# Output products of two feed-forward stages: earlier scalings, additions spread over the steps, a fourth weight buffer, and the last tile in two banks

## The chip, the cores and the metric

One core of a Trainium2 chip runs the whole kernel. The metric is the time of one execution on the device in microseconds, the median of several runs. The core has five engines that run beside each other and wait for one another by semaphores: TensorE (PE in the profile, with its weight loads as PEld), VectorE (DVE), ScalarE (ACT), GpSimd (POOL) and SyncE (SP). SP only issues DMAs here, in order, from one queue; a DMA whose buffer isn't free yet holds up those behind it.

## The reference

One layer of a hybrid model: 512 tokens of width 1024, feed-forward width 2816, all in float32.

```python
mod = jax.nn.silu(c) @ w_ada + b_ada
sh1, sc1, g1, sh2, sc2, g2, sh3, sc3, g3 = [m[:, None, :] for m in jnp.split(mod, N_MOD, axis=-1)]

u = rms_norm(x, ffn1_norm_g) * (1 + sc1) + sh1
x = x + 0.5 * g1 * swiglu(u, ffn1_w_in, ffn1_w_out)     # swiglu: (silu(a) * b) @ w_out, [a b] = u @ w_in
...
x = x + g2 * (merged @ w_out)                           # mLSTM and attention with a forget gate, merged
u = rms_norm(x, ffn2_norm_g) * (1 + sc3) + sh3
x = x + 0.5 * g3 * swiglu(u, ffn2_w_in, ffn2_w_out)
```

The change concerns the two products with `ffn1_w_out` and `ffn2_w_out` (512 x 2816 by 2816 x 1024), and the line that scales their results by 0.5 g and adds them onto x. The two stages are called FFN1 and FFN2 below.

## The kernel before

**Exactness.** TensorE multiplies a rounded kind of float32. So every operand is split in a high half (`wh`, `A`: a copy by ScalarE, L102 for weights) and a low half (`wl`, `Ra`, `Rb`, `Rl`: what is left, a subtraction by VectorE, L104 for weights). One product is three matmuls, `mm3`: high by high (L127), high by low (L128 and L129, named for their place, each with one low half). In the rows, L128 of the output products reads `wl` and L129 a low half of the activations.

**The output product.** `pair_out` computes h @ w_out with seven products for a 2 x 2 block of matrices instead of eight (Strassen and Winograd's scheme). The 22 blocks of 128 rows of w_out form NP = 11 pairs, and sums of weight blocks that the scheme needs stand ready in DRAM (`ws`). There are two sweeps over the pairs.

The first sweep sums three products in PSUM banks and ends with P1 = the first of them, U2 = P1 + the second (L573) and U4 = U2 + the third (L575), each for two tiles of 128 tokens (`tb` 0 and 1), 128 x 512. These six tiles belong to the result: scaled by 0.5 g they are added onto x.

The second sweep sums four products, Z and Y in banks named t, X and W in banks named g, each for two values of tb. It has 8 steps, one for each of pairs 0 to 7, of 24 matmuls. A step needs two weight tiles of 128 x 1024 (512 KB): `c` out of w_out for Z and Y, and `d` out of `ws` for X and W. Each is loaded by SP into a buffer `raw` (there are 3, used in turn, L92), and split by ScalarE into `wh` and by VectorE into `wl` (4 buffers each). After that, pairs 8, 9 and 10 (`tail = 3`) are done bank by bank: `close` does the remaining 9 matmuls of one bank, so that the banks are finished one after the other and not all at the end. Their d tiles are loaded early, in steps 3, 5 and 7, into buffers that are free by then (`early`, `we`, L544 to L546); their c tiles, c8 to c10, follow behind step 7's in the raw buffers.

**x.** It has four tiles of 128 tokens by two halves of 512 columns. They are loaded in the source's steps 3 to 6 (L621), two a step, from the input in FFN1 and from `x_d` in FFN2. In the source's steps 6 and 7, P1, U2 and U4 are scaled (`scaled`, L597, into a buffer `rs`) and added (`onto`, L600), U4's onto two tiles. When a bank is closed, its sum is scaled and added likewise (X's onto both halves of its tile).

**The end of the stages.** FFN1 hands `pair_out` a function `end`, which closes the banks in an order written by hand and goes on to the next normalization. FFN2 closes X, Z, W and Y in a loop over "XZYW" (X, Z, Y, W), tb 0 and 1 each, and stores each finished tile of 128 x 512 (256 KB, L607): eight stores, the last after W, tb = 1.

**What sets the order.** A scheduler (the Tile framework's) orders the instructions of each engine by the program's dependences and its own estimates; each engine then runs its list in order. So the source's order is a starting point, and the same change of the source can move other instructions too. The buffer named `xn` (one, 128 x 1024) holds the activations' rest `R` of the last pair in FFN1, until L482 has split it, and in FFN2 a sum that a side computation (`ada_row`) builds up until about 1126 us.

Of the kernel before, what the change touches and what calls it, by code (L numbers as in the profile page):

```python
# [11 lines left out]
F32 = mybir.dt.float32  # L12
# [8 lines left out]
P = 128  # L21
# [23 lines left out]
MUL, ADD, SUB, MAX, MIN = ALU.mult, ALU.add, ALU.subtract, ALU.max, ALU.min  # L45


class Layer:
# [478 lines left out]
    def pair_out(self, w, v, hp, tp, x_src, end=None):  # L527

        nc = self.nc
        V = nc.vector.tensor_tensor  # L530
        NP = NJ // 2
        slots = iter([f"{a}{k}" for k in range(NK) for a in ("uh", "ul")])
        new = lambda n: self.up.tile([P, 512], F32, name=self.nm(n), tag=next(slots))
        sh = [P, 2, 512]
        def two(*src):

            n = 2 // len(src)
            t = self.raw(sh, [(lambda t, i=i: t[:, i:i + n, :] if n > 1 else t[:, i, :], a) for i, a in enumerate(src)])
            return self.split(t, sh)
        def early(src, n):  # L540

            hi, lo = [hp.tile(sh, F32R, name=self.nm("we"), tag=f"A{n + i}", bufs=1) for i in range(2)]
            t = lo.bitcast(F32)
            nc.sync.dma_start(t, src)  # L544
            nc.scalar.activation(hi, t, AF.Copy)
            V(lo, t, hi, op=SUB)  # L546
            return hi, lo
        both = lambda r: w[r * P:(r + 1) * P, :].rearrange("p (h n) -> p h n", h=2)
        def one(src):
            t = self.tmp(tp, "raw1")  # L550
            nc.sync.dma_start(t, src)
            return self.split(t, [P, 512])
        def mm(ps, tb, a, b, start, stop):
            s = slice(tb * P, (tb + 1) * P)
            self.mm3(ps[tb], a[0][:, s], a[1][:, s], b[0], b[1], start, stop)

        Z, Y = [[self.tbank() for _ in range(2)] for _ in range(2)]
        X = [self.gbank() for _ in range(2)]
        for i in range(NP):
            wh, wl = two(w[2 * i * P:(2 * i + 1) * P, 0:512], self.ws[i][:, 0, :])  # L560
            w2 = one(self.ws[i][:, 3, :])
            self.tick()
            A1 = self.A1[i]
            for ps, n, b in ((Z, 0, (wh[:, 0, :], wl[:, 0, :])), (X, 2, w2), (Y, 1, (wh[:, 1, :], wl[:, 1, :]))):
                for tb in range(2):
                    mm(ps, tb, (A1[:, n, :], A1[:, 3 + n, :]), b, i == 0, i == NP - 1)
            if i:
                self.pair_split(i - 1, hp, tp)
        P1, U2, U4 = [[new(n) for _ in range(2)] for n in ("P1", "U2", "U4")]
        for tb in range(2):  # L570
            nc.scalar.activation(P1[tb], Z[tb], AF.Copy)
        for tb in range(2):
            V(U2[tb], X[tb], P1[tb], op=ADD)  # L573
        for tb in range(2):
            V(U4[tb], Y[tb], U2[tb], op=ADD)  # L575
        self.pair_split(NP - 1, hp, tp)

        X, W = [[self.gbank() for _ in range(2)] for _ in range(2)]
        Z, Y = [[self.tbank() for _ in range(2)] for _ in range(2)]
        banks = {"Z": Z, "Y": Y, "X": X, "W": W}  # L580
        def prepare(i, d=None):
            c = two(both(2 * i + 1))
            d = d or two(self.ws[i][:, 1:3, :])
            A2 = self.A2[i]
            a = lambda n: (A2[0][:, n, :], A2[1 + n // 2][:, n % 2, :])
            b = lambda n: ((c, d)[n // 2][0][:, n % 2, :], (c, d)[n // 2][1][:, n % 2, :])
            return {"Z": (a(0), b(0)), "Y": (a(3), b(1)), "X": (a(2), b(2)), "W": (a(1), b(3))}
        step = lambda n, tb, i, o: mm(banks[n], tb, *o[n], i == 0, i == NP - 1)
        if end:
            g = [self.mod_bcast(v, h, tp) for h in range(2)]  # L590
        else:
            g = [new("gb") for _ in range(2)]
            for h in range(2):
                nc.sync.dma_start(g[h], self.mod_d[v:v + 1, h * 512:(h + 1) * 512].to_broadcast([P, 512]))
        def scaled(src, half, t=None):
            t = self.tmp(tp, "rs") if t is None else t
            self.pin(nc.vector.scalar_tensor_tensor(t, src, 0.5, g[half], op0=MUL, op1=MUL))  # L597
            return t
        def onto(tb, half, t):
            self.pin(V(self.x[tb][half], self.x[tb][half], t, op=ADD))  # L600
        def add(src, half, tbs):
            t = scaled(src, half)
            for tb in tbs:
                onto(tb, half, t)
            return t
        def store(tb, half):
            nc.sync.dma_start(self.out[0, tb * P:(tb + 1) * P, half * 512:(half + 1) * 512], self.x[tb][half])  # L607
        tail, ds = 3, []
        for i in range(NP - tail):
            o = prepare(i)  # L610
            if i % 2 and i > 1:
                n = NP - tail + len(ds)
                ds.append(early(self.ws[n][:, 1:3, :], i - 3))
            for n in ("XZWY" if i == 0 else "ZYXW"):
                for tb in range(2):
                    step(n, tb, i, o)
            if i == 3:
                self.x_tiles()
            if 3 <= i < 7:
                for h in range(2):  # L620
                    nc.sync.dma_start(self.x[i - 3][h], x_src[(i - 3) * P:(i - 2) * P, h * 512:(h + 1) * 512])  # L621
            if i in (6, 7):
                tb = i - 6
                add(P1[tb], 0, (tb,))
                add(U2[tb], 0, (tb + 2,))
                add(U4[tb], 1, (tb, tb + 2))
        def close(n, tb):
            ps = banks[n][tb]
            for i, o in enumerate(os):
                step(n, tb, NP - tail + i, o)  # L630
            return ps
        place = lambda n, tb: {"Z": (0, tb), "Y": (1, tb), "W": (0, tb + 2)}[n]
        os = [prepare(NP - tail + n, d) for n, d in enumerate(ds)]
        if end:
            end(close, scaled, onto)
            return

        for n in "XZYW":
            for tb in range(2):
                ps = close(n, tb)  # L640
                if n == "X":
                    add(ps, 1, (tb + 2,))
                    add(ps, 0, (tb + 2,))
                    store(tb + 2, 1)
                else:
                    half, q = place(n, tb)
                    add(ps, half, (q,))
                    store(q, half)
# [940 lines left out]
```

## Time and profile before

| | us |
|---|---|
| median of 3 runs | 1327.01 |
| lowest and highest | 1326.8 and 1328.08 |
| profiled execution | 1328.68 |
| its span in the profile | 1326.9 |
| second sweep, FFN1: first matmul | 315.13 |
| second sweep, FFN2: first matmul | 1260.44 |
| last matmul, start | 1321.69 |
| last store, issue | 1323.6 |

The granted clock of TensorE is 1.0 over the span. A row of a timeline has the start in us, the duration in us, the engine, the line, the operation, out<-in with names less their numbers, the shapes, and in brackets the idle time of the engine ahead of it with what ended it. A row can hold several equal instructions in sequence (x2, x3); its duration then covers them all. On TensorE consecutive matmuls overlap, so their pace is read from the starts. A row of a group has, behind the bar, the busy time in us and the mean in ns of one, and behind a second bar the idle time of the engine just ahead. A row of DMA issues has the count, the size of one, and the median us from issue to landing.

### The profile page before, as it was taken

The page shows a single profiled execution, that of the slowest core. Times are in us where ns is not written, and L with a number is a line of the kernel's source. Part 1 is how long each engine was busy: PE and PEld are TensorE (multiplying, and loading weights), DVE is VectorE, ACT ScalarE, POOL GpSimd, SP SyncE. Part 2 cuts the span into 40 slices and gives each one's busy share as a digit, 9 for nine tenths or more (in the row PEclk, how much of TensorE's full clock was granted, in tenths as well). Part 3 has the DMA queues.
Part 4 walks back from the last instruction along what each step waited for, and adds up shares of the span by engine and source line. Part 5 has one row for each costly group of instructions (what it writes and reads, how often), then busy time and mean ns, then how long its engine had stood idle before and what let it go on. Part 6 is the DMA issues. An engine that isn't in the chain of part 4 may idle for free.

```text
span 1326.9 us, 17767 instructions
## 1 busy us (share of the span) xinstructions
PE 1308.3 (99%) x6332; PEld 1091.9 (82%) x6332; DVE 959.9 (72%) x1740; ACT 622.6 (47%) x1038; POOL 43.8 (3%) x65
## 2 busy tenths in 40 slices
PE   7999999999999999999999999999999999999998
PEld 6788888888789888888888788888788888888886
DVE  6877777467788687887887778677577656635777
ACT  5533232355476555566566666334263223223742
POOL 1000000000010101000000000003010000000000
PEclk9999999999999999999999999999999999999999
DMA  9899978464845334533342536687429768624574
GB/s 291 265 325 306 315 269 280 127 194 155 291 133 139 110 108 130 159 103 111 91 122 76 170 96 204 214 256 227 155 92 339 264 235 277 210 97 140 170 260 152
DMA packets 204345, 254.18 MB, mean 192 GB/s; under 512 B 14993, under 2 KB 146481, under 8 KB 204257
## 3 DMA queue, kind: packets, MB, share of 16 engines
q1 hardware_dynamic: 203872, 252.98, 59.9%
q8 instruction: 50, 0.82, 0.2%
q14 instruction: 39, 0.31, 0.1%
q0 software_dynamic: 320, 0.06, 0.0%
q10 hardware_dynamic: 64, 0.02, 0.0%
HBM read 217.28 MB, written 35.72 MB: 191 GB/s over the span
## 4 chain that ended last, share of the span: by engine, by line
PE 91%; DVE 4%; ACT 2%; DMA 2%; issue 1%; POOL 0%; SPq 0%; ACTq 0%; DVEq 0%; POOLq 0%
PE g L127 23%; PE g L129 23%; PE g L128 23%; PE t L128 4%; PE t L127 4%; PE t L129 4%; PE g L825 2%; PE t L1208 1%; PE t L1178 1%; DMA x<-x_d 1%; DVE wl L104 1%; PE t L1149 1%; PE t L825 1%; PE t L1150 1%; ACT wh L102 0%
## 5 line engine op out<-in xcount | busy, mean ns | idle before, releaser
L102 ACT ACTIVATE wh<-raw 128x1024 fp32r<-128x1024 f32 (+2 forms) x250 | 253.9, 1018 | 383.0 <-PE g L128 118.4
L104 DVE TENSOR_TENSOR wl<-raw,wh 128x1024 fp32r<-128x1024 f32 (+2 forms) x250 | 292.9, 1174 | 178.0 <-ACT wh L102 154.8
L128 PE MATMUL g<-ul,wh 128*128 128x512 f32 (+1 forms) x912 | 348.1, 383 | 1.0 <-POOL ul L267 1.0
L127 PE MATMUL g<-uh,wh 128*128 128x512 f32 (+1 forms) x912 | 348.5, 384 | 0.0
L129 PE MATMUL g<-uh,wl 128*128 128x512 f32 (+1 forms) x912 | 348.2, 382 | 0.0
L128 PEld LDWEIGHTS g<-ul,wh 128*128 128x128 f32 x912 | 171.3, 188 | 34.3 <-POOL ul L267 1.8
L129 PEld LDWEIGHTS g<-uh,wl 128*128 128x128 f32 x912 | 171.4, 188 | 33.2
L127 PEld LDWEIGHTS g<-uh,wh 128*128 128x128 f32 x912 | 171.0, 188 | 32.8 <-issue 0.6
L325 DVE SCALAR_TENSOR_TENSOR acc<-raw,ccol,acc 128x512 f32<-128x512 f32 (+1 forms) x70 | 66.8, 975 | 43.0 <-DMA raw<-in_w_ada_dram 42.6
L127 PE MATMUL g<-wh,uh 128*128 128x512 f32 (+1 forms) x256 | 97.4, 380 | 0.0
L129 PE MATMUL g<-wh,ul 128*128 128x512 f32 (+1 forms) x256 | 96.6, 377 | 0.0
L128 PE MATMUL g<-wl,uh 128*128 128x512 f32 (+1 forms) x256 | 96.4, 377 | 0.0
L128 PE MATMUL t<-wl,A 128*128 128x512 f32 x176 | 69.3, 394 | 1.7 <-DVE wl L104 1.6
L127 PE MATMUL t<-wh,A 128*128 128x512 f32 x176 | 69.3, 394 | 0.1
L129 PEld LDWEIGHTS g<-wh,ul 128*128 128x128 f32 x256 | 48.2, 188 | 9.0
L127 PEld LDWEIGHTS g<-wh,uh 128*128 128x128 f32 x256 | 48.2, 188 | 8.7 <-DVE tk L1046 0.5
L128 PEld LDWEIGHTS g<-wl,uh 128*128 128x128 f32 x256 | 48.2, 188 | 8.3
L127 PE MATMUL g<-yh,wh 128*128 128x512 f32 x128 | 50.4, 394 | 0.0
L129 PE MATMUL g<-yh,wl 128*128 128x512 f32 x128 | 50.2, 392 | 0.0
L128 PE MATMUL g<-yl,wh 128*128 128x512 f32 x128 | 49.7, 388 | 0.0
L455 ACT ACTIVATE A<-E 128x768 fp32r<-128x768 f32 x22 | 18.6, 846 | 56.5 <-DVE E L454 50.6
L1160 ACT ACTIVATE S<-S,mn 128x128 f32<-128x128 f32 (+1 forms) x64 | 35.5, 556 | 16.1 <-DVE mn L1152 9.9
(343 smaller groups left out, 2187.5 us busy)
## 6 DMA issues: line engine op xcount, KB each, us to landing
raw<-in_ffn_w_in_dram SPq DMA_DIRECT2D x82, 512.0 KB, 5.2
raw<-in_w_ada_dram SPq DMA_DIRECT2D x56, 512.0 KB, 5.1
raw<-in_w_mix_dram SPq DMA_DIRECT2D x46, 512.0 KB, 4.3
sa<-in_ffn_w_out_dram SPq DMA_DIRECT2D x22, 512.0 KB, 5.4
sb<-in_ffn_w_out_dram SPq DMA_DIRECT2D x44, 256.0 KB, 5.9
ws<-sa SPq DMA_DIRECT2D x22, 512.0 KB, 4.5
ws<-sb SPq DMA_DIRECT2D x44, 256.0 KB, 4.1
raw<-ws SPq DMA_DIRECT2D x44, 256.0 KB, 3.4
```

Source lines behind the costliest of these rows:

```text
L102: nc.scalar.activation(hi, src, AF.Copy)
L104: self.last_lo = nc.vector.tensor_tensor(lo, src, hi, op=SUB)
L127: pin(mm(ps, lh, rh, start=start, stop=False))
L128: pin(mm(ps, lh, rl, start=False, stop=False))
L129: self.last_mm = pin(mm(ps, ll, rh, start=False, stop=stop))
L325: nc.vector.scalar_tensor_tensor(a, r[:, s], c, a, op0=MUL, op1=ADD)
L455: nc.scalar.activation(A1[:, 0:3, :], E[:, 0:3, :], AF.Copy)
L825: pin(nc.tensor.matmul(acc_ps[b], (wl if p == 1 else wh)[:, b % 2, s], self.ul[k] if p == 2 else self.uh[k], start=k == 0 and p == 0, stop ...
L1149: nc.tensor.matmul(ps[:, :w], q[:, s], k[:, :w], start=True, stop=False)
L1150: nc.tensor.matmul(ps[:, :w], q[:, s], kl[:, :w], start=False, stop=True)
L1160: nc.scalar.activation(S[:, ws], S[:, ws], AF.Exp, scale=-1.0, bias=m, accum_out=sm[:, qb:qb + 1])
L1178: tr = lambda b, c, qb, kb: nc.tensor.transpose(b[:, c:c + P], S[:, P_OFF[qb] + kb * P:P_OFF[qb] + (kb + 1) * P], self.ident)
```

## The change

1. A fourth buffer. For odd pairs, the d tile goes into the buffer `xn` (`two_x`) and no longer into a raw buffer. Even d tiles and all c tiles keep the three raw buffers.
2. P1, U2 and U4 are scaled in place in steps 0, 1 and 2, two operations a step. From step 4 on, each step adds two of them onto x: step i onto the two halves of the token tile i - 4.
3. In FFN2 only: bank W of tb = 1 ends after step 7 and is scaled and added onto its tile of x ahead of the closings. Its remaining three pairs are done last, in two new banks of 256 columns each, with a scaling, an addition and a store (128 KB) of their own. These are 18 matmuls of 256 columns in place of 9 of 512.

In all TensorE gets 9 instructions more, VectorE 4 and SP one store; ScalarE and GpSimd keep theirs.

```diff
+        def two_x(src):
+            t = tp.tile(sh, F32, name=self.nm("raw"), tag="xn", bufs=1)
+            nc.sync.dma_start(t, src)
+            return self.split(t, sh)
...
-        banks = {"Z": Z, "Y": Y, "X": X, "W": W}
+        banks, tail = {"Z": Z, "Y": Y, "X": X, "W": W}, 3
...
-            d = d or two(self.ws[i][:, 1:3, :])
+            d = d or (two_x if i % 2 else two)(self.ws[i][:, 1:3, :])
...
-        step = lambda n, tb, i, o: mm(banks[n], tb, *o[n], i == 0, i == NP - 1)
+        step = lambda n, tb, i, o: mm(banks[n], tb, *o[n], i == 0, i == NP - (1 if end or n != "W" or not tb else 1 + tail))
...
-            if i in (6, 7):
-                tb = i - 6
-                add(P1[tb], 0, (tb,))
-                add(U2[tb], 0, (tb + 2,))
-                add(U4[tb], 1, (tb, tb + 2))
+            for src, half in ((P1, 0), (U2, 0), (U4, 1))[i:i + 1]:
+                for tb in range(2):
+                    scaled(src[tb], half, src[tb])
+            if i >= 4:
+                tb = i - 4
+                onto(tb, 0, (P1, U2)[tb // 2][tb % 2])
+                onto(tb, 1, U4[tb % 2])
...
+        add(W[1], 0, (3,))
         for n in "XZYW":
             for tb in range(2):
+                if n == "W" and tb:
+                    for c in (slice(0, 256), slice(256, 512)):
+                        ps, x, r = self.gbank((P, 256)), self.x[3][0][:, c], slice(P, 2 * P)
+                        for i, o in enumerate(os):
+                            a, b = o[n]
+                            self.mm3(ps, a[0][:, r], a[1][:, r], b[0][:, c], b[1][:, c], i == 0, i == tail - 1)
+                        t = self.tmp(tp, "rs")[:, :256]
+                        nc.vector.scalar_tensor_tensor(t, ps, 0.5, g[0][:, c], op0=MUL, op1=MUL)
+                        V(x, x, t, op=ADD)
+                        nc.sync.dma_start(self.out[0, 3 * P:4 * P, c], x)
+                    continue
                 ps = close(n, tb)
```

The lines behind the change move by 4 to 18: what was L546 is L550, L597 is L601, L600 is L604, L621 is L625; `two_x` loads at L542, and the last tile's two parts are scaled at L654, added at L655 and stored at L656.

Three places show what this does to the engines' lists. Names carry numbers here that tell the tiles apart.

VectorE in FFN2's second sweep, steps 5 and 6, before. `wl_11907` is the low half of d5, `wl_11944` that of c6, `wl_11950` that of d6; `we` is an early d tile, `x_11854` and `x_11855` are the halves of token tile 2, and `x_11853`, `x_11856` and `x_11857` those of tiles 1 and 3.

```order
L104 TENSOR_TENSOR wl_11907<-raw_11904,wh_11906 128x1024
L600 TENSOR_TENSOR x_11854<-x_11854,rs_11982 128x512
L546 TENSOR_TENSOR we_11911<-we_11911,we_11910 128x1024
L600 TENSOR_TENSOR x_11855<-x_11855,rs_11985 128x512
L597 TENSOR_SCALAR rs_12036<-U_2228_11675,gb_11698 128x512
L600 TENSOR_TENSOR x_11853<-x_11853,rs_12036 128x512
L104 TENSOR_TENSOR wl_11944<-raw_11941,wh_11943 128x1024
L600 TENSOR_TENSOR x_11856<-x_11856,rs_12033 128x512
L104 TENSOR_TENSOR wl_11950<-raw_11947,wh_11949 128x1024
```

The same place now, where d5, c6 and d6 are `wl_11909`, `wl_11948` and `wl_11954`:

```order
L104 TENSOR_TENSOR wl_11909<-raw_11906,wh_11908 128x1024
L104 TENSOR_TENSOR wl_11948<-raw_11945,wh_11947 128x1024
L550 TENSOR_TENSOR we_11913<-we_11913,we_11912 128x1024
L604 TENSOR_TENSOR x_11854<-x_11854,U_2219_11666 128x512
L604 TENSOR_TENSOR x_11855<-x_11855,U_2221_11668 128x512
L604 TENSOR_TENSOR x_11857<-x_11857,U_2222_11669 128x512
L104 TENSOR_TENSOR wl_11954<-raw_11951,wh_11953 128x1024
L604 TENSOR_TENSOR x_11856<-x_11856,U_2220_11667 128x512
```

c6 has moved ahead of the early tile and of all additions; three additions stand between it and d6. In step 4 likewise one addition stands ahead of c4's `wl` (two of them and the early tile before), and two more and the early tile between c4's and d4's.

TensorE at the start of FFN1's second sweep, before; `wl_2801` is d0's low half, `wl_2795` c0's, g_2780 and g_2781 are X's banks, t_2784 is Z's first.

```order
L127 MATMUL g_2780<-wh_2800,A_444_2406 128x512
L127 MATMUL g_2781<-wh_2800,A_444_2406 128x512
L127 MATMUL t_2784<-wh_2794,A_444_2406 128x512
L128 MATMUL t_2784<-wl_2795,A_444_2406 128x512
L129 MATMUL t_2784<-wh_2794,Rl_2407 128x512
```

And now:

```order
L127 MATMUL g_2780<-wh_2800,A_444_2406 128x512
L127 MATMUL g_2781<-wh_2800,A_444_2406 128x512
L127 MATMUL t_2784<-wh_2794,A_444_2406 128x512
L128 MATMUL g_2780<-wl_2801,A_444_2406 128x512
L129 MATMUL g_2780<-wh_2800,Rl_2407 128x512
```

The low half of d0 is read by the fourth matmul; before, it was the eighteenth. FFN2's sweep begins in the same order now.

SP's queue in FFN1, the loads of steps 1 to 3, before: c1, d1, c2, d2, c3, d3.

```order
L92 DMA raw_2828<-in_ffn_w_out_dram 128x1024
L92 DMA raw_2834<-ws_742 128x1024
L92 DMA raw_2864<-in_ffn_w_out_dram 128x1024
L92 DMA raw_2870<-ws_743 128x1024
L92 DMA raw_2900<-in_ffn_w_out_dram 128x1024
L92 DMA raw_2906<-ws_744 128x1024
```

And now:

```order
L92 DMA raw_2830<-in_ffn_w_out_dram 128x1024
L92 DMA raw_2868<-in_ffn_w_out_dram 128x1024
L92 DMA raw_2874<-ws_743 128x1024
L542 DMA raw_2836<-ws_742 128x1024
L92 DMA raw_2906<-in_ffn_w_out_dram 128x1024
L542 DMA raw_2912<-ws_744 128x1024
```

d1 (`raw_2836`) has gone behind c2 and d2, and c3 stands behind it.

More of the change, by code (lines that the diff above doesn't have):

```diff
@@ L607, in store @@
             nc.sync.dma_start(self.out[0, tb * P:(tb + 1) * P, half * 512:(half + 1) * 512], self.x[tb][half])
-        tail, ds = 3, []
+        ds = []
         for i in range(NP - tail):
```

## The prediction

> **What bounds the kernel now.** I began with the page's first and fourth parts: how busy each engine is, and which engine the chain of waits runs through.
>
> ```profile
> PE 1308.3 (99%) x6332; PEld 1091.9 (82%) x6332; DVE 959.9 (72%) x1740; ACT 622.6 (47%) x1038; POOL 43.8 (3%) x65
> PE 91%; DVE 4%; ACT 2%; DMA 2%; issue 1%; POOL 0%; SPq 0%; ACTq 0%; DVEq 0%; POOLq 0%
> L128 PE MATMUL t<-wl,A 128*128 128x512 f32 x176 | 69.3, 394 | 1.7 <-DVE wl L104 1.6
> ```
>
> TensorE sets the end: 99% busy, 91% of the chain. The change adds a little to it and removes nothing from it, so it can only gain where TensorE waits, and behind its last matmul. The groups by line show a wait in the output products: the matmuls of L128 on the t banks idle for VectorE's low half `wl` (third row; L127 is high by high, L128 uses `wl`). That sum counts idle time alone. What a stall costs is the gap between the starts of two matmuls, less the steady gap. TensorE's timeline around the two stalls of FFN2's second sweep:
>
> ```profile
> 1282.26 0.39 PE L127 MATMUL t<-wh,A 128*128 128x512 f32 x1
> 1282.78 0.50 PE L128 MATMUL t<-wl,A 128*128 128x512 f32 x1
> 1283.12 0.40 PE L129 MATMUL t<-wh,Ra 128*128 128x512 f32 x1
> ...
> 1293.61 0.39 PE L127 MATMUL t<-wh,A 128*128 128x512 f32 x1
> 1294.79 0.50 PE L128 MATMUL t<-wl,A 128*128 128x512 f32 x1 [0.80 <-DVE wl L104]
> ```
>
> Undisturbed, matmuls of this sweep start 0.227 us apart (1321.01 to 1321.69 are three gaps, in the rows of the tail below). At c4 (step 4) the second matmul starts 0.52 behind the first, and the third 0.34 behind that: 0.29 + 0.11 = 0.40 lost. At c6 it is 1.18 - 0.227 = 0.95, with the same 0.11 for the restart 1.06. FFN2 loses 1.46 us. VectorE's timeline says why:
>
> ```profile
> 1278.46 0.69 DVE L600 TENSOR_TENSOR x<-x,rs 128x512 f32<-128x512 f32 x1 [1.47 <-DMA x<-x_d]
> ...
> 1281.50 1.23 DVE L104 TENSOR_TENSOR wl<-raw,wh 128x1024 fp32r<-128x1024 f32 x1
> ...
> 1289.84 0.69 DVE L600 TENSOR_TENSOR x<-x,rs 128x512 f32<-128x512 f32 x1 [0.63 <-DMA x<-x_d]
> 1290.45 1.22 DVE L546 TENSOR_TENSOR we<-we,we 128x1024 fp32r<-128x1024 f32 x1
> ...
> 1293.52 1.22 DVE L104 TENSOR_TENSOR wl<-raw,wh 128x1024 fp32r<-128x1024 f32 x1
> ```
>
> VectorE works in order. Ahead of c4's `wl` (1281.50) and c6's (1293.52) stand additions onto x that wait for a load of x, 1.47 and 0.63 us. In front of c6 the run from 1289.84 to 1293.52 is four 0.69 operations on x and one 1.22 split; `wl` ends at 1294.74, TensorE starts at 1294.79.
>
> FFN1's second sweep loses its time at c10, the last weight tile: TensorE, VectorE, SP's queue and ScalarE.
>
> ```profile
> 360.63 0.39 PE L127 MATMUL t<-wh,A 128*128 128x512 f32 x1
> ...
> 361.10 0.40 PE L129 MATMUL t<-wh,Ra 128*128 128x512 f32 x1
> 361.56 0.50 PE L127 MATMUL t<-wh,A 128*128 128x512 f32 x1
> 362.82 0.50 PE L128 MATMUL t<-wl,A 128*128 128x512 f32 x1 [0.76 <-DVE wl L104]
> ...
> 350.44 6.77 SPq L92 DMA_DIRECT2D raw<-in_ffn_w_out_dram  x3
> ...
> 355.62 1.23 DVE L104 TENSOR_TENSOR wl<-raw,wh 128x1024 fp32r<-128x1024 f32 x1 [2.79 <-ACT wh L102]
> 356.82 1.23 DVE L546 TENSOR_TENSOR we<-we,we 128x1024 fp32r<-128x1024 f32 x1
> 361.54 1.22 DVE L104 TENSOR_TENSOR wl<-raw,wh 128x1024 fp32r<-128x1024 f32 x1 [0.89 <-ACT wh L102]
> ...
> 360.44 1.06 ACT L102 ACTIVATE wh<-raw 128x1024 fp32r<-128x1024 f32 x1 [1.05 <-DMA raw<-in_ffn_w_out_dram]
> ```
>
> Here the steady gap is 0.233 (two from 360.63 to 361.10). The gaps of 0.46 and 1.26 and the restart lose 0.23 + 1.03 + 0.10 = 1.36 us. Backwards: c10's `wl` starts 361.54, its `wh` 360.44 after a wait for the load. SP's row covers the loads of c8, c9 and c10, from 350.44 to 357.21; the last is issued at 356.87, right behind d7's `wl` (355.62 + 1.23), because d7 holds the raw buffer that c10 takes.
>
> The tail, TensorE, VectorE and the stores:
>
> ```profile
> 1321.01 0.39 PE L129 MATMUL g<-we,Ra 128*128 128x512 f32 x1
> ...
> 1321.69 0.39 PE L129 MATMUL g<-we,Ra 128*128 128x512 f32 x1
> 1322.12 0.69 DVE L597 SCALAR_TENSOR_TENSOR rs<-g,gb 128x512 f32<-128x512 f32 x1 [0.62 <-PE g L129]
> 1322.84 0.69 DVE L600 TENSOR_TENSOR x<-x,rs 128x512 f32<-128x512 f32 x1
> ...
> out_dram<-x SPq DMA_DIRECT2D x8, 256.0 KB, 2.0
> ```
>
> From the last matmul's end (1322.08) to the span's end (1326.9) pass 4.82 us: a scaling and an addition of 0.69 each, the store's 2.0 and the small steps between them.
>
> **The change part by part.**
>
> *FFN2's stalls.* c6's `wl` now stands ahead of every addition of its step (front part, VectorE's order), and only one addition stands ahead of c4's. The scalings between them are gone from there. So neither tile waits for x ahead of its `wl`, or only behind one addition: gain 1.46. From the other side: three additions now stand ahead of d4's and of d6's `wl`. TensorE uses a d tile only 12 matmuls (2.7 us) into a step, so 1.47 of waiting for x fits there. Bounds 0 to -1.46; I take -1.46: the tile that is needed first no longer queues behind the load that comes last.
>
> *FFN1's stall.* With d7 in the fourth buffer, c10 takes c7's raw buffer. c7's split is over some 4 us before d7's (d7's `wl` waited 2.79 us), so the load is issued about 353 and is there in time. Then VectorE binds: from 355.62 it still has d7, early d10, c8, c9 and c10 to split, at 1.2 each, and c10 ends at 355.62 + 4 x 1.20 + 1.23 = 361.65. Undisturbed TensorE needs it at 361.56. Some 0.15 of the stall is left if d7's `wl` stays where it is: -1.2. Bounds 0 (the chain is not shortened) and -1.36.
>
> *New margins at the sweep's start.*
>
> ```profile
> 313.17 0.69 DVE L597 SCALAR_TENSOR_TENSOR rs<-P,gb 128x512 f32<-128x512 f32 x1
> 313.77 1.28 DVE L573 TENSOR_TENSOR U<-g,P 128x512 f32<-128x512 f32 x2
> 315.83 0.39 PE L128 MATMUL t<-wl,A 128*128 128x512 f32 x1
> ...
> 316.76 0.69 DVE L482 TENSOR_TENSOR Rb<-R,A 128x512 fp32r<-128x512 f32 x1
> 318.65 0.33 SPq L92 DMA_DIRECT2D raw<-in_ffn_w_out_dram  x1
> 322.20 1.06 ACT L102 ACTIVATE wh<-raw 128x1024 fp32r<-128x1024 f32 x1 [4.76 <-DMA raw<-in_ffn_w_out_dram]
> 324.47 0.39 PE L128 MATMUL g<-wl,A 128*128 128x512 f32 x1
> ```
>
> TensorE's new order needs d0's `wl` as its fourth matmul, which is at 315.83. The scaling at 313.17 goes, the two U2 move up 0.6 to end at 314.4, and `wl` behind them ends at 315.7: just in time, 0 to +0.2. d1 is now loaded into the buffer of R's last pair, free only when that is split. By these rows this ends at 317.45; one `wl` (1.22) now comes before it and a scaling (0.6) no longer does, so about 318.1. A load here took 3.55 from issue to use (318.65, 322.20): there at 321.8, `wh` to 322.9, `wl` to 324.1, needed at 324.47. 0 to +0.5. In FFN2 that buffer has long been idle, so there d1 comes earlier than now. I take +0.1 for all of this.
>
> *Work that only moves.* Six scalings a sweep (0.69 each) go into its steps 0 to 2, two a step, behind the `wl` that TensorE needs next; their number stays. FFN2 adds W[1]'s scaling and addition ahead of X's reading on VectorE, 1.38 us. They can start when step 7 is over, and X's first closing takes 9 x 0.227 = 2.04 after that, so they are covered: 0. Without the cover X is read and stored up to 1.4 later, which the closings of Z, W and Y (some 12 us) hide again. SP issues one store more, behind all others.
>
> *The tail.* Nine matmuls of 512 columns become eighteen of 256. Matmuls of 256 columns run in the mix stage, and VectorE has operations of half the size; below them a store of 128 KB from the page's DMA issues:
>
> ```profile
> 399.24 0.28 PE L1398 MATMUL g<-uh,wl 128*128 128x256 f32 x1
> 399.36 0.28 PE L1397 MATMUL g<-uh,wh 128*128 128x256 f32 x1
> ...
> L751 DVE SCALAR_TENSOR_TENSOR ac<-ar,ccol,ac 128x256 f32<-128x256 f32 x49 | 23.7, 483 | 1.3
> L457 DVE TENSOR_TENSOR Rb<-E 128x256 f32<-128x256 f32 x21 | 8.9, 422 | 0.4
> ...
> h_d<-hn SPq DMA_DIRECT2D x16, 128.0 KB, 1.8
> ```
>
> At 0.12 apart they take 2.16 instead of 2.04: +0.12. Each has its own weight load; on average one takes 1091.9 / 6332 = 0.172, and if nothing hid it the eighteen would take 3.10, +1.06. I take the row of the same shape, where the loads are hidden. VectorE's 0.69 + 0.69 becomes 0.48 + 0.42: -0.48. The last store halves; 256 KB landed in 2.0 (above), 128 KB elsewhere in 1.8: -0.2, bounds 0 and -1.0. Together -0.56, bounds +0.58 and -1.36.
>
> The Trainium skill ("TensorE: Matmul & The Clock Gate", section "Back-to-back issue gap") has a stream of weight load and matmul at some 81 ns for 128 columns and 131 ns for 512. Between them, an estimate from that page, 256 columns stand at about 98 ns: 1.76 for the eighteen against 1.18 for the nine, +0.58 in place of +0.12, which would make the time 1324.4. The trace doesn't agree with its 512-column figure (0.227 here against 0.131), so I keep the rows.
>
> *Sum.* -1.46 - 1.2 + 0.1 - 0.56 = -3.1. The profiled execution took 1328.68 us (span 1326.9, 1.78 around it), 1.67 above the median of the three runs. The steps have the same lengths in both, so I take the sum off the median: 1327.01 - 3.1 = **1323.9**. What a measurement can tell from no change here is about 0.2%, 2.65 us: faster means below 1324.36.
>
> **The rivals.**
>
> *FFN1 gives it back.* The fifth split in VectorE's row of splits binds, or c10's load arrives late all the same. For it: the split is ready 0.1 us late as it is, and three loads come close upon each other from 350 on. Against it: c10's load gets 4 us. Then 1327.01 - 1.46 + 0.1 - 0.56 = 1325.1.
>
> *The x wait moves.* d4's or d6's `wl` waits behind three additions whose x comes late. For it: VectorE waited 1.47 for x, and weight loads of 512 KB are issued around the loads of x. Against it: 2.7 us of slack. It would keep FFN2's 1.46: 1325.4.
>
> *Single fourth buffer, slower.* Every second d tile goes through one buffer. d3 can't be requested until d1's `wl` is done, at 324.1, and is needed two steps of 24 matmuls later, 324.47 + 11.2 = 335.7. Less 1.06 and 1.22 for the splits this leaves 9.3 us for the load, which also stands in SP's queue behind the loads ahead of it.
>
> ```profile
> raw<-ws SPq DMA_DIRECT2D x7, 512.0 KB, 7.2
> ```
>
> These are the loads of d in FFN2's second sweep (DMA issues of that stretch): 7.2 us in the median, 2 us in hand. For it: a median leaves half of them above it. It decides from 9.3 us on: at 11 us d3, d5 and d7 would each stall 1.7 in both sweeps, +10.2 - 3.1, about 1334; at 10.5 about 1331.
>
> **How the numbers follow.** The forecast has 0.60, with a range of its own of 1323.1 to 1324.8; about eight tenths of that (0.48) lie under 1324.36. FFN1 gives it back 0.18, the x wait moves 0.13: both within 0.2%. The single buffer has 0.08, slower. The last 0.01 is a larger gain. So faster 0.49, same 0.43, slower 0.08. For 8 in 10: 1322.8 (tail at its best bound) to 1326.0, which leaves out the single buffer and a second failed term.
>
> **What would show it.** TensorE's timeline: no gap over 0.3 at c4, c6 and c10; the group of L128 on the t banks idle near 0.1 instead of 1.7. SP: c10's load issued about 353 in FFN1. VectorE: no wait for `x_d` ahead of a `wl` that TensorE needs next. The last 18 matmuls 0.12 apart and about 4.1 us from their end to the span's. Gaps at L128 on the g banks, on odd steps, would speak for the single buffer; one at FFN1's step 1 for the late d1. Were the second sweeps as long as before with these gaps closed, the reading of the bound would be wrong.

## The result, and the profile after

| | before | changed |
|---|---|---|
| median of 22 runs, us | 1327.66 | 1325.23 |
| lowest to highest, us | 1325.45 to 1329.57 | 1324.66 to 1327.27 |
| ratio, with its 95% interval | | 0.9983 (0.9977 to 0.9989) |
| profiled execution, us | 1328.68 | 1325.80 |
| its span, us | 1326.9 | 1324.0 |

The ratio is 2.3 us of 1327.66, with an interval of 1.5 to 3.1: faster, but by less than the 0.2% that the prediction set as its bound, and 0.8 less than the 3.1 it forecast. In these runs the changed kernel also spreads less.

The page and the group of L128 on the t banks, changed kernel:

```profile
PE 91%; DVE 4%; ACT 2%; DMA 1%; issue 1%; POOL 0%; ACTq 0%; POOLq 0%; DVEq 0%
L128 PE MATMUL t<-wl,A 128*128 128x512 f32 x176 | 69.1, 393 | 0.0
```

The idle time before that group was 1.7 us and is 0. TensorE's timeline of the changed kernel at the three places, c10 in FFN1, c4 and c6 in FFN2:

```profile
360.81 0.39 PE L127 MATMUL t<-wh,A 128*128 128x512 f32 x1
361.04 0.40 PE L128 MATMUL t<-wl,A 128*128 128x512 f32 x1
...
1281.63 0.39 PE L127 MATMUL t<-wh,A 128*128 128x512 f32 x1
1281.85 0.39 PE L128 MATMUL t<-wl,A 128*128 128x512 f32 x1
...
1292.51 0.39 PE L127 MATMUL t<-wh,A 128*128 128x512 f32 x1
1292.73 0.39 PE L128 MATMUL t<-wl,A 128*128 128x512 f32 x1
```

Gaps of 0.23, 0.22 and 0.22, the steady pace; before they were 1.26, 0.52 and 1.18. One small gap is new, at the start of FFN2's second sweep, at d0's low half:

```profile
1260.07 0.39 PE L127 MATMUL t<-wh,A 128*128 128x512 f32 x1
1260.41 0.50 PE L128 MATMUL g<-wl,A 128*128 128x512 f32 x1
1260.74 0.39 PE L129 MATMUL g<-wh,Rl 128*128 128x512 f32 x1
```

Gaps of 0.34 and 0.33 instead of 0.227: 0.22 lost, where the prediction gave 0 to 0.2. FFN1's sweep starts with half of that, 0.10.

The tail: of the kernel before, TensorE's first matmul of the last tile; of the changed kernel, TensorE's first and last matmul of the split tile, VectorE's last two operations, and the two stores (time to issue, first and last issue):

```profile
1319.88 0.39 PE L127 MATMUL g<-we,A 128*128 128x512 f32 x1
...
1317.67 0.28 PE L127 MATMUL g<-we,A 128*128 128x256 f32 x1
1319.70 0.28 PE L129 MATMUL g<-we,Ra 128*128 128x256 f32 x1
...
1320.02 0.42 DVE L654 SCALAR_TENSOR_TENSOR rs<-g,gb 128x256 f32<-128x256 f32 x1
1320.47 0.42 DVE L655 TENSOR_TENSOR x<-x,rs 128x256 f32<-128x256 f32 x1
...
L656 SPq DMA_DIRECT2D out_dram<-x x2: 332/332/332, 1320.1 to 1320.9; - x2
```

Seventeen gaps of the changed kernel take 2.03 us, 0.12 each. From the first of its matmuls here to the span's end pass 1324.0 - 1317.67 = 6.33 us. Before, the last tile began at 1319.88 and the span ended at 1326.9: 7.02. The tail gained 0.69.

One stall in the changed kernel's trace was not in the one of before, in the merge of the two branches, whose code the change doesn't touch. TensorE and ScalarE there:

```profile
888.40 0.39 PE L128 MATMUL g<-yl,wh 128*128 128x512 f32 x1
889.32 0.50 PE L129 MATMUL g<-yh,wl 128*128 128x512 f32 x1 [0.53 <-DVE wl L104]
...
886.95 1.06 ACT L102 ACTIVATE wh<-raw 128x1024 fp32r<-128x1024 f32 x1 [1.17 <-DMA raw<-in_w_branch_b_dram]
```

The second matmul starts 0.92 behind the first: 0.69, and 0.11 with the restart, are lost, because a load of w_branch_b came late. Is it the change's doing? That, and which part of the change did what, is left to the experiments.

### The profile page after: what moved, and what is told of

The parts are those of the page before. It is cut to its first block, busy times and chain, and to the rows that moved or that the text cites. A ratio compares the mean times of both kernels' runs of the same rounds, so it can differ in the third digit from the quotient of the medians.

```text
span 1324.0 us, 17792 instructions
## 1 busy us (share of the span) xinstructions
PE 1308.0 (99%) x6341; PEld 1092.2 (82%) x6341; DVE 959.9 (73%) x1744; ACT 623.7 (47%) x1038; POOL 43.7 (3%) x65
## 4 chain that ended last, share of the span: by engine, by line
PE 91%; DVE 4%; ACT 2%; DMA 1%; issue 1%; POOL 0%; ACTq 0%; POOLq 0%; DVEq 0%
PE g L129 23%; PE g L127 23%; PE g L128 23%; PE t L127 4%; PE t L129 4%; PE t L128 4%; PE g L843 2%; PE t L1226 1%; PE t L1196 1%; PE t L1167 1%; PE t L843 1%; PE t L1168 1%; DVE wl L104 1%; DMA raw<-in_w_branch_b_dram 0%; ACT wh L102 0%
## 5 line engine op out<-in xcount | busy, mean ns | idle before, releaser
L128 PE MATMUL g<-ul,wh 128*128 128x512 f32 (+1 forms) x912 | 348.1, 383 | 1.0 <-POOL ul L267 1.0
L128 PEld LDWEIGHTS g<-ul,wh 128*128 128x128 f32 x912 | 171.3, 188 | 34.3 <-POOL ul L267 1.8
L128 PE MATMUL g<-wl,uh 128*128 128x512 f32 (+1 forms) x256 | 96.4, 377 | 0.0
L128 PE MATMUL t<-wl,A 128*128 128x512 f32 x176 | 69.1, 393 | 0.0
L128 PEld LDWEIGHTS g<-wl,uh 128*128 128x128 f32 x256 | 48.2, 188 | 8.3
L128 PE MATMUL g<-yl,wh 128*128 128x512 f32 x128 | 49.7, 388 | 0.0
```

Source lines behind the costliest of these rows:

```text
L128: pin(mm(ps, lh, rl, start=False, stop=False))
```

## The experiments

Below, a stall is what TensorE's gaps between starts exceed the steady pace by, summed over gaps of more than 0.07 us excess, in the two second sweeps and in the merge (up to 893 us). Each row is one profiled execution; the ratio is that of the timed runs to runs of the kernel before on the same chip.

| kernel | FFN1 | merge | FFN2 | ratio (95% interval) |
|---|---|---|---|---|
| before | 1.36 | 0 | 1.47 | |
| before, again | 0.80 | 0 | 0.69 | 1.0001 (0.9992 to 1.0010) |
| split tail alone | 0 | 0.65 | 0.83 | 0.9993 (0.9984 to 1.0002) |
| spread additions alone | 1.22 | 0.34 | 1.16 | 0.9993 (0.9984 to 1.0001) |
| changed, no buffer | 0.89 | 1.51 | 0.53 | 0.9991 (0.9982 to 0.9999) |
| fourth buffer alone | 0.09 | 1.17 | 0 | 0.9983 (0.9974 to 0.9992) |
| changed, no spread | 0.68 | 3.76 | 0 | 0.9988 (0.9979 to 0.9997) |
| changed, no split | 0.11 | 0.12 | 0.22 | 0.9992 (0.9983 to 1.0001) |
| changed | 0.10 | 0.80 | 0.22 | 0.9983 (0.9977 to 0.9989) |
| changed, again | 0.11 | 0 | 0.22 | 0.9980 (0.9972 to 0.9989) |
| changed, third | 0.68 | 0.59 | 0.22 | 0.9987 (0.9978 to 0.9995) |
| buffer from d3, split tail | 0 | 4.03 | 0 | 0.9985 (0.9976 to 0.9994) |
| buffer from d3, rest as changed | 0.11 | 0.94 | 0.23 | 0.9987 (0.9979 to 0.9996) |

An interval of 0.0009 to either side is 1.2 us, as much as a part is worth. The times alone don't tell the parts apart (0.9980 to 0.9992 with the buffer, 0.9991 to 1.0001 without it); what a part does inside is read from the profiles.

**The fourth buffer alone.**

```diff
+        def two_x(src):
+            t = tp.tile(sh, F32, name=self.nm("raw"), tag="xn", bufs=1)
+            nc.sync.dma_start(t, src)
+            return self.split(t, sh)
...
-            d = d or two(self.ws[i][:, 1:3, :])
+            d = d or (two_x if i % 2 else two)(self.ws[i][:, 1:3, :])
```

> The kernel before with the fourth buffer for the d tiles of odd pairs alone. Theory: c10 in FFN1 no longer waits (1.36 us), while FFN2's stalls at c4 and c6 (1.46) are made by additions that stand ahead of wl in VectorE's list and stay or shrink a little; d1 in FFN1 comes later, up to 1 us lost at step 1. Time 0.5 to 1.4 us below before. Rival: x comes late because SP's queue is held up by full raw buffers, so the buffer alone removes c4 and c6 too: 2.5 to 3 us below before.

Measured: no stall at c10, none at c4 and none at c6; 0.9983, 1.1 to 3.5 us below before. The rival holds. The additions still stand ahead of c6's low half, as SP, ScalarE, VectorE and TensorE of this kernel show:

```profile
1277.15 1.45 SPq L92 DMA_DIRECT2D raw<-in_ffn_w_out_dram  x1
...
1284.44 1.06 ACT L102 ACTIVATE wh<-raw 128x1024 fp32r<-128x1024 f32 x1 [0.21 <-DMA raw<-in_ffn_w_out_dram]
...
1286.85 0.69 DVE L604 TENSOR_TENSOR x<-x,rs 128x512 f32<-128x512 f32 x1
1287.46 1.22 DVE L104 TENSOR_TENSOR wl<-raw,wh 128x1024 fp32r<-128x1024 f32 x1
...
1291.91 0.39 PE L127 MATMUL t<-wh,A 128*128 128x512 f32 x1
1292.13 0.39 PE L128 MATMUL t<-wl,A 128*128 128x512 f32 x1
```

`wl` stood some 2 us behind ready data (1285.50 to 1287.46) and was finished 3.4 us before TensorE used it. VectorE's order costs nothing when the load is early. Now the rows of the kernel before that the prediction didn't read, SP's issue of c6 and ScalarE's `wh` of c4 and c6:

```profile
1284.60 0.40 SPq L92 DMA_DIRECT2D raw<-in_ffn_w_out_dram  x1
...
1280.40 1.06 ACT L102 ACTIVATE wh<-raw 128x1024 fp32r<-128x1024 f32 x1 [1.80 <-DMA raw<-in_ffn_w_out_dram]
1291.82 1.06 ACT L102 ACTIVATE wh<-raw 128x1024 fp32r<-128x1024 f32 x1 [2.14 <-DMA raw<-in_ffn_w_out_dram]
```

c4's `wh` ended at 1281.46 and its `wl` began at 1281.50: whatever stood ahead of it on VectorE cost 0.04 us. c6's `wh` ended at 1292.88, its `wl` began at 1293.52, so the additions right ahead of it cost 0.64 at most. The rest was a load that was asked for at 1284.60, was used 7.2 us later, and could not be asked for before d4's raw buffer was split. With the buffer it is issued at 1277.15.

**The spread additions alone.**

```diff
-            if i in (6, 7):
-                tb = i - 6
-                add(P1[tb], 0, (tb,))
-                add(U2[tb], 0, (tb + 2,))
-                add(U4[tb], 1, (tb, tb + 2))
+            for src, half in ((P1, 0), (U2, 0), (U4, 1))[i:i + 1]:
+                for tb in range(2):
+                    scaled(src[tb], half, src[tb])
+            if i >= 4:
+                tb = i - 4
+                onto(tb, 0, (P1, U2)[tb // 2][tb % 2])
+                onto(tb, 1, U4[tb % 2])
```

> The kernel before with the early scalings and the two additions a step alone. Theory: FFN2's stalls at c4 and c6 go (1.46), FFN1's at c10 stays (its load still waits for d7's split): about 1.4 us below before. Rival (the buffer does it all): c4 and c6 still stall, 0 to 0.3 us below before.

Measured: c4's stall is gone, c6's isn't, d0 costs 0.2, FFN1 stands as it did: 0.9993, not told from no change. c4's stall is absent as well in two further executions of the old order (the split tail alone, and the kernel before again, both below), so the new order isn't shown to have removed it. VectorE and SP at d4's split, then ScalarE, VectorE and TensorE at c6:

```profile
1282.33 0.69 DVE L600 TENSOR_TENSOR x<-x,P 128x512 f32<-128x512 f32 x1 [0.69 <-DMA x<-x_d]
1282.94 1.22 DVE L104 TENSOR_TENSOR wl<-raw,wh 128x1024 fp32r<-128x1024 f32 x1
...
1282.82 1.02 SPq L621 DMA_DIRECT2D x<-x_d  x2
1284.19 0.33 SPq L92 DMA_DIRECT2D raw<-in_ffn_w_out_dram  x1
...
1292.01 1.06 ACT L102 ACTIVATE wh<-raw 128x1024 fp32r<-128x1024 f32 x1 [1.66 <-DVE we L546]
...
1293.10 1.23 DVE L104 TENSOR_TENSOR wl<-raw,wh 128x1024 fp32r<-128x1024 f32 x1 [0.60 <-ACT wh L102]
...
1293.33 0.40 PE L127 MATMUL t<-wh,A 128*128 128x512 f32 x1
1294.38 0.50 PE L128 MATMUL t<-wl,A 128*128 128x512 f32 x1 [0.66 <-DVE wl L104]
```

At c6 VectorE now waits idle for `wh`, and TensorE stalls all the same: what is late is the load. The new order even holds that load up a little. An addition that waits for x now stands ahead of d4's `wl`; this ends at 1284.16, and only then can SP ask for c6, at 1284.19, 0.35 after its issues before that were over (1283.84). Neither theory fits as written: c6's stall stays, and c4's proves nothing.

**The split tail alone.**

```diff
-        step = lambda n, tb, i, o: mm(banks[n], tb, *o[n], i == 0, i == NP - 1)
+        step = lambda n, tb, i, o: mm(banks[n], tb, *o[n], i == 0, i == NP - (1 if end or n != "W" or not tb else 1 + tail))
...
+        add(W[1], 0, (3,))
...
+                if n == "W" and tb:
+                    for c in (slice(0, 256), slice(256, 512)):
...
+                    continue
```

> The kernel before with the last tile in two banks alone. Theory: from the last matmul to the end of the span 0.7 to 0.8 us less, matmuls 0.12 more, all other stalls as before: 0.6 us below before. Rival (the store's and the end's fixed parts set it): within 0.2 us of before.

Measured: the tail as in the changed kernel (from the last matmul's start to the span's end 1324.2 - 1319.95 = 4.25, 5.21 before); 0.9993, which is 0.9 us with an interval that reaches past 0. The surprise is in the table. Every engine's list of this kernel is the same as before's up to FFN2's closings. Yet FFN1's stall at c10, 1.36 in the execution the prediction read, is 0 here, and the merge has the stall that came up in the changed kernel's trace. So a stall at either place can come or go without any change of the instructions.

**The changed kernel again, and a third time.** No edit.

> The changed kernel once more, unchanged. It shows whether its wait of 0.5 us (0.8 to 1.0 with the restart) at w_branch_b's low half near 889 us, which the kernel before did not show, belongs to it: if it is there again, the change gave back about 0.9 us outside the two products; if it is not, it was one execution's chance, and this execution is some 0.9 us shorter there. Time 2.0 to 2.6 us below before either way.

> The changed kernel a third time, beside the two above on the same chip. Theory: stalls of 0.1 and 0.2 us in the two second sweeps again, and at w_branch_b anything from 0 to 1 us by chance; 2.0 to 2.4 us below before.

Measured: 0.9980 and 0.9987, or 2.7 and 1.7 us, the first a little more and the second less than was expected. The stall in the merge is 0 in one and 0.59 in the other. The stall of 0.22 at FFN2's d0 is there each time. In the third, FFN1 loses 0.57 more at step 1, where it was to lose nothing (ScalarE and TensorE):

```profile
322.13 3.90 ACT L102 ACTIVATE wh<-raw 128x1024 fp32r<-128x1024 f32 x4 [6.21 <-DMA raw<-ws]
...
323.24 1.19 PE L127 MATMUL g<-wh,A 128*128 128x512 f32 x4
324.50 0.50 PE L128 MATMUL g<-wl,A 128*128 128x512 f32 x1
```

That is d1, loaded late into the buffer of R's last pair, as the prediction feared with 0 to 0.5: 0 in two executions, 0.57 in one.

**The kernel before, again.** No edit.

> The kernel before once more, unchanged. Theory: the stall of 1.36 us at c10 in FFN1 was the chance of one execution whose load of d7 landed late (issue to use 6.3 us, where the kernel with the split tail alone, same code there, had 4.2 and no stall): here it is gone or smaller than 0.5, while c4 and c6 in FFN2 stall again by about 0.4 and 1. Rival: the stall at c10 belongs to the kernel and stands here again with over 1 us. Time as before.

Measured: neither as written; c10 stalls by 0.80, c6 by 0.69, c4 not at all. SP's issue of d7 and ScalarE's `wh` of it, first of this kernel, then of the one with the split tail alone:

```profile
347.10 0.33 SPq L92 DMA_DIRECT2D raw<-ws  x1
352.58 1.06 ACT L102 ACTIVATE wh<-raw 128x1024 fp32r<-128x1024 f32 x1 [2.19 <-DMA raw<-ws]
```

```profile
347.76 0.33 SPq L92 DMA_DIRECT2D raw<-ws  x1
352.00 1.06 ACT L102 ACTIVATE wh<-raw 128x1024 fp32r<-128x1024 f32 x1 [1.66 <-DMA raw<-ws]
```

and of the execution that the prediction read:

```profile
348.26 0.33 SPq L92 DMA_DIRECT2D raw<-ws  x1
...
354.53 1.06 ACT L102 ACTIVATE wh<-raw 128x1024 fp32r<-128x1024 f32 x1 [2.95 <-PE g L129]
```

The same instructions, and from the issue of d7's load to its use 5.5, 4.2 and 6.3 us, with stalls at c10 of 0.80, 0 and 1.36. (The last row names TensorE as what ended the wait; by its place in the other two it was the load.) In these three the stall follows the time that the load takes, and that varies.

**All but one part.** First without the buffer, then without the spread additions, then without the split tail; the edits are those above, undone one at a time.

```diff
-            d = d or (two_x if i % 2 else two)(self.ws[i][:, 1:3, :])
+            d = d or two(self.ws[i][:, 1:3, :])
```

> The changed kernel without the fourth buffer (early scalings, spread additions and the split tail stay). Theory, as the earlier runs suggest: FFN2's stalls at c4 and c6 are late loads that only the buffer brings forward, so c6 still stalls 0.8 to 1.0 us; the rest gives 0.7 (tail) and 0 to 0.7 (order): 0.7 to 1.4 us below before, some 1 us behind the changed kernel. Rival (VectorE's order, as predicted): c4 and c6 go without the buffer, as fast as the changed kernel.

```diff
-            for src, half in ((P1, 0), (U2, 0), (U4, 1))[i:i + 1]:
-                for tb in range(2):
-                    scaled(src[tb], half, src[tb])
-            if i >= 4:
...
+            if i in (6, 7):
+                tb = i - 6
+                add(P1[tb], 0, (tb,))
...
```

> The changed kernel without the early scalings and spread additions (the buffer and the split tail stay). Theory: with the weights loaded earlier the order of VectorE's additions costs nothing, and the 0.2 us that the changed kernel loses at d0 at the start of FFN2's second sweep is not lost here: as fast as the changed kernel or 0.2 to 0.4 faster, 2.2 to 2.8 below before. Rival (order and buffer are both needed): 0.5 to 1 us behind the changed kernel.

```diff
-        add(W[1], 0, (3,))
...
-                if n == "W" and tb:
...
-                    continue
```

> The changed kernel with its last tile in one bank again (buffer, scalings and additions stay). Theory: 0.7 us behind the changed kernel, 1.4 to 1.8 below before; from the last matmul's start to the end of the span 5.2 again. Rival (the tail was worth nothing): as fast as the changed kernel.

Measured: without the buffer 0.9991, stalls in both sweeps, as the theory had it, though c6's was only 0.31 in this execution, where 0.8 to 1.0 was expected; the rival, that the order suffices, falls. Here SP asked for c6 0.65 later than it could have, again because of d4's split, so that an order which spares d4 too might have removed these 0.31; no run tried one. Without the spread additions no stall in FFN2, not even d0's 0.22, but d1 late by 0.68 in FFN1; 0.9988, not told from the changed kernel's 0.9983. So the spread takes 0.2 from FFN2. That it gives FFN1 anything isn't shown: the fourth buffer alone, whose lists are the same there, lost 0.09, and the changed kernel lost 0.57 at d1 in its third execution. Without the split 0.9992, from the last matmul's start to the span's end 5.2 again, as expected.

**The buffer from d3 on.** First with the split tail and the additions as before, then in the changed kernel.

```diff
-            d = d or (two_x if i % 2 else two)(self.ws[i][:, 1:3, :])
+            d = d or (two_x if i % 2 and i > 1 else two)(self.ws[i][:, 1:3, :])
```

> Fourth buffer for the odd d tiles from d3 on only, the split tail, and the additions as before (no early scalings). Theory: c4, c6 and c10 get their loads early, d1 keeps its early load in a raw buffer, and d0 is read late as before, so no stall over 0.1 us in either second sweep: 0.3 us less than the changed kernel's 0.3 of stalls, 2.3 to 2.8 below before. Rival (the additions must be spread when the buffer starts late): 0.3 to 1 us of stalls at c4 or c6.

> The changed kernel, but the fourth buffer takes the odd d tiles only from d3 on. Theory: stalls as in the changed kernel, 0.1 in FFN1 and 0.2 in FFN2 at d0; d1 was not what cost time there: as the changed kernel within 0.2 us. Rival: d1's late load also held back later tiles, 0.3 us faster.

Measured: the first has no stall in either second sweep, as expected, the only kernel here with none. Its time, 0.9985, isn't told from the changed kernel's 0.9987 beside it, since the 0.3 to 0.9 us are smaller than what a run's chance adds. In this execution that was 4.03 us in the merge. The second has the changed kernel's stalls, 0.11 and 0.23, and its time. A version that is shown to beat the changed kernel was not found.

## Why the prediction was right, and where not

The time of 1325.23 lies in the stated range, and the direction was right. The size was not: 2.3 us instead of 3.1. By the prediction's own bound of 0.2% that is "same", to which it gave 0.43, and not the "faster" that it gave 0.49. Of the 1.3 us between 1323.9 and 1325.23, 0.65 is the base: the kernel before has its median at 1327.66 over 22 runs and had it at 1327.01 over three.

*FFN2's stalls, predicted -1.46.* The step that failed reads "Ahead of c4's `wl` (1281.50) and c6's (1293.52) stand additions onto x that wait for a load of x", and takes the gain from the new order of VectorE. It followed one of the two things that the late `wl` waits for, its place in VectorE's list. The other, `wh`, was nearly as late: ready 0.04 and 0.64 us before `wl` began. The loads were late because SP couldn't issue them without a raw buffer; the fourth buffer alone has neither stall with the additions in place, and the order alone leaves c6's. Over all runs c6 stalls in each of the five executions without the buffer, by 0.31 to 1.06 us, and in none of the eight with it. The prediction also weighed the additions ahead of d4's `wl` only against TensorE's need of d4 (2.7 us of slack), not against c6, which without the fourth buffer waits for d4's raw buffer. The stall did go, by the other part of the change; that this term came out with the right sign is luck. Its size was a sample: the same instructions lost 1.47, 0.69 and 0.83 us in three executions, 1.0 in the mean. The changed kernel loses 0.22 at d0 each time. Gain 0.8.

*FFN1's stall, predicted -1.2.* The mechanism was right: with d7 out of the raw buffers c10 is loaded early, and c10 never stalls in a kernel with the buffer. The size was wrong for the same reason: 1.36, 0.80 and 0 in three executions of the same list, 0.72 in the mean. Against this the changed kernel has 0.10, 0.11 and 0.68, mean 0.30. Gain 0.42. The 0.15 us that were to remain at c10 (five splits in a row on VectorE) didn't: d7's load is earlier too, so the row began earlier.

*Margins at the sweep's start, predicted +0.1.* They came out as 0.10 (d0) and up to 0.57 (d1, just over its bound of 0.5) in FFN1 and 0.22 in FFN2; they are in the sums above.

*The tail, predicted -0.56.* Measured -0.69. The scaling of 128 x 256 took 0.42 and not the 0.48 of the row it was taken from. The pace of 0.12 was right. The figures of the Trainium skill ("TensorE: Matmul & The Clock Gate", section "Back-to-back issue gap"), by whose estimate the eighteen would have cost 0.58 more than the nine, don't agree with these runs: 0.12 us where the estimate was 0.098 for 256 columns, and 0.227 for 512 where the page has 0.131.

*The sum.* 0.8 + 0.42 + 0.69 = 1.91, inside the measured interval of 1.5 to 3.1; with three executions a side, whose stalls range as widely as they do, that is weak support. The stall in the merge is chance as far as the split tail's run shows (0.65 with unchanged lists). That it is as frequent in all kernels isn't shown: it was 0 in three of thirteen executions, two of them of the kernel before.

*The rivals.* The single fourth buffer never held a d tile late from d3 on; 2 us in hand were enough. The wait for x did move: in the changed kernel d4's `wl` (1280.95) stands behind an addition that waited 0.85 us for x. TensorE shows no gap there, so the slack was enough. In gain, what came true (2.3 us) lies between the forecast's 3.1 and the 1.9 of "FFN1 gives it back".

## What to carry to other kernels

When an operation is late, look at when each of its inputs was ready before blaming what stands ahead of it in its queue: the difference between the last input and its start is all that a new order can give it directly. Then ask who waits for the buffers of the operations that the new order puts back. A stall that hangs on a load's landing is a sample. One trace gave 1.36 us for something that the same program does with 0 to 1.36, and a gain read from it should be cut accordingly, or read from several. A buffer more helps by letting the queue ask earlier; what it removes shows on kernels with that part alone, not in the sum.

## What the runs showed of the hardware

Loads of 512 KB took 4.2, 5.5 and 6.3 us from issue to use at one and the same place of the same program.

In two executions the merge cost far more than the stall itself. The windows of the kernel with the buffer from d3 on and the split tail (columns: the stretch, its length, busy time of PE, PEld, DVE, ACT and POOL with counts, granted clock, DMA share, GB/s), and TensorE in it:

```profile
881.00:884.00 3.00, 2.53 (x9) 1.22 (x7) 2.01 (x4) 0.96 (x2) 0.00 (x0) 1.00 0.72 267
884.00:890.00 6.00, 4.80 (x14) 3.88 (x15) 3.91 (x7) 1.58 (x2) 1.58 (x1) 0.72 0.79 247
890.00:900.00 10.00, 10.00 (x46) 7.95 (x45) 7.65 (x11) 2.75 (x3) 2.48 (x2) 1.00 0.78 229
```

```profile
883.55 0.40 PE L128 MATMUL g<-yl,wh 128*128 128x512 f32 x1
885.20 0.79 PE L129 MATMUL g<-yh,wl 128*128 128x512 f32 x1 [1.25 <-DVE wl L104]
885.79 0.63 PE L127 MATMUL g<-yh,wh 128*128 128x512 f32 x1
886.22 0.63 PE L128 MATMUL g<-yl,wh 128*128 128x512 f32 x1
886.64 0.63 PE L129 MATMUL g<-yh,wl 128*128 128x512 f32 x1
```

After a gap of 1.65 us, with two shorter ones before it, the matmuls start 0.43 apart instead of 0.23, and the granted clock of that stretch is 0.72. The other execution (changed, no spread) shows the same after the same gap. The gap of 1.26 at c10 in the kernel before was followed by the old pace. The Trainium skill, "TensorE: Matmul & The Clock Gate", section "HAM oscillation — how this bites in real kernels", tells of a clock that falls to half when waits of some 3 to 5 us for loads leave TensorE idle. The pace here agrees with the half; the idle time doesn't agree, with 1.25 us at the longest and two shorter ones before it. The 1.42 us lost in this gap became about 3 with what followed. The kernel before may have such executions too: of its 29 runs beside this kernel's, two took 1332.16 and 1330.08 us at a mean granted clock of 0.997 and 0.998, but where in them the clock fell isn't recorded.
